# A state-space and attention block on one core: a first stage by half tiles, and all queries ahead of the state-space quarters

## The chip, the cores and the metric

The kernel runs on one core of a Trainium2 chip. The core has five engines with a queue of instructions each: PE (TensorE, the matrix multiplier; its weight loads are listed as PEld), DVE (VectorE), ACT (ScalarE), POOL (GpSimd) and SP (SyncE, which here starts the DMA transfers). An engine works off its own queue in order and waits for others by semaphores. The metric is the device time of one execution, in microseconds (us); less is better.

## The reference, cut to what matters

One transformer-like layer on 512 tokens of width 1024, in float32:

```python
n1 = rmsnorm(h, g_mix)                 # h: 512 x 1024
z = n1 @ w_in                          # columns: ssm 512 | q 512 | kv 768 | gates 24 | merge 2048
y_ssm = s5_mixer(z[..., OFF_SSM:OFF_Q], ...)    # 32 groups of 16 channels, 64 complex states each
y_nsa = nsa_mixer(z[..., OFF_Q:OFF_KV], ...)    # attention: compressed, selected and window branch
merge = sigmoid(z[..., OFF_MERGE:])
mixed = merge[..., :1024] * (y_ssm @ w_br_ssm) + merge[..., 1024:] * (y_nsa @ w_br_nsa)
h = h + mixed @ w_out
h = h + conv_ffn(rmsnorm(h, g_ffn), w_up, conv_w, conv_b, w_down)   # 2 x 2816 wide
gate = sigmoid(rmsnorm(h, g_ple) @ w_ple_gate)
h = h + gate * (p @ w_ple_proj)        # p: 512 x 256, the embedding
return rmsnorm(h, g_final)
```

`s5_mixer` is a linear recurrence over the tokens, `state = a_bar * state + B u`, `y = Re(C state) + d u`, where `a_bar = exp(lambda * dt)` is complex; then come a gelu and a gated product with `w_glu`.

## The kernel before, in words

**Precision.** TensorE multiplies operands in the type fp32r. Each large product is therefore made of three: an operand is split in a high part (a copy to fp32r, on ACT, the function `copy`) and a low part (operand minus high part, on DVE or POOL, the function `tt` with SUB, line L54), and high x high, low x high and high x low are added up in one PSUM bank. So whatever TensorE multiplies needs first an ACT copy and then a subtraction, and the third kind of pass is the one that needs the low weights.

**Memory.** PSUM has eight banks, two each under four names ("acc", "s", "t", "o"). Raw weights of a projection (`wr`, 128x1024) have three buffers, their high and low parts (`wh`, `wl`) two each: splitting a third weight waits until TensorE has finished with the first.

**Who orders what.** Up to L506 the four compute engines follow the order in which the code is written (the block under `tc.manual_schedule`). From there a scheduler orders the instructions of each engine when the program is built; `tc.issue_after(x)` holds work back until instruction x, and the stage leaves such marks: `trig_at` (the last angle operation on DVE), `exp_at` (POOL's last instruction so far) and `zero_at` (ACT's last gate and value copy). DMAs are issued on SP's queue in the order of the code.

**First stage (L240 to L506).**
- *Warm-up*: 12 float32 matmuls of 128x128 without a use for their result. A float32 matmul is two passes, so the trace shows 24.
- *Embedding*: `p @ w_ple_proj` in two halves of 512 columns (`embedded(i, qt)`: half i, 128 tokens qt; six matmuls of 128x512 each, `pje`). `pT` holds the high and low parts of p, `wp[i]` those of half i of the weights (`wpr` raw). `embedded_out` copies a result to SBUF, and later a DMA takes it to DRAM, since it is needed only at the end.
- *Normalization of x*, four tiles of 128 tokens (qt = 0 to 3). `xload(qt)` loads the tile twice: as rows (`rows[qt]`, for the sum of squares) and transposed (`xT`). `squared` is the sum of squares on ACT, `rooted` the power -0.5 on POOL (two instructions, `rx`), `spread` a matmul that spreads the 128 roots over all partitions (`rb`), `x_scaled` eight DVE operations of 128x128 that multiply xT by the gain and by `rb`, `n_high` the high part on ACT (`n1h`, 128x1024) and `n_low` the low part on DVE (`n1l`).
- *Values and gates*: `v_passes(qt, passes)` multiplies a tile with 280 columns of w_in, eight matmuls for each of the three kinds of pass (`vps`). The weights `WV` come in two pieces of 128 and 152 columns (`wv(x, i)`, low parts by `wv_lo`). `v_out` takes the result out: tanh for the gates, high part, low part.
- *Angles*: `angled` is a chain of small DVE operations (128x16, up to 14 of them an exponential) that prepares the state-space parameters; `some(n)` issues the next n of it.
- `u_split` splits the weights of the first two projections.

Row 0 of x lies in one half of a buffer (`wv_101` in the rows below, [:, 1]) whose other half takes the first value weights.

**Projections and quarters.** A projection (`proj`, lines L82 to L84) is 24 matmuls of 128x512 into a bank `pj`. There are four for the state space (`un`; each result goes to DRAM and back in another layout, `ud` and `Uc`), four for the queries (`queries(i)`, result `QT`), then keys and the inputs of the compressed branch. Each needs `wh` and `wl` of one weight block of 512 KB.

The state space is worked off in four quarters of eight groups (`ssm_quarter(q)`). Each makes products of powers and parameters on DVE (`z`) and POOL (`x`), which ACT places in `Z` and `CX`; TensorE transposes Z (`wbps`), ACT copies that (`WB`); TensorE multiplies with `Uc` (`wps`); DVE turns and scans the result (`sr`, with the decay `dec` and the table `tab` that POOL and ACT make once, L631); TensorE makes `tps` out of Z and CX and the output `yps` out of both. Z and CX have two sets of buffers, which alternate between quarters.

Later stages are attention, the state space's gated product (`glu`), merge, FFN and gate. Their code is the same in both kernels.

Of the kernel before, what the change touches and what calls it, by code (L numbers as in the profile page):

```python
# [18 lines left out]
P = 128  # L19
# [25 lines left out]
def hybrid_kernel(ctx: ExitStack, tc: tile.TileContext, A, out):  # L45
# [194 lines left out]

    def xload(qt):
        nc.sync.dma_start(rows[qt], dr("x", qt * P * D, [[D, P], [1, D]]))
        nc.sync.dma_start(xT[:, qt], dr("x_t", qt * P * D, [[D, P], [P, KD], [1, P]]))
# [14 lines left out]
    nc.sync.dma_start(cols, dr("cols", 0, [[NCOLS, P], [1, NCOLS]]))  # L258
    for k in range(2):
        wpload(1, k)  # L260
# [7 lines left out]
    for qt in range(1, NQ):  # L268
        xload(qt)
# [22 lines left out]
    def v_out(qt):  # L292
        ps = vps[qt]
        vv = VV[:, qt].rearrange("p b g x d -> p (b g) x d")
        x = ps[:, 0:256].rearrange("p (a d) -> p a d", d=HD)
        S.activation(gates[:, qt], ps[:, 256:280], AF.Tanh, scale=0.5)
        copy(vv[:, :, 0], x)
        ts(gates[:, qt], gates[:, qt], 0.5, 0.5, MUL, ADD, G)
        tt(vv[:, :, 1], x, vv[:, :, 0], SUB)
# [17 lines left out]
    def x_scaled(qt):  # L317
        for k in range(KD):
            stt(xT[:, qt, k], xT[:, qt, k], gmix[:, k:k + 1], rbp[0][:, qt * P:(qt + 1) * P], MUL, MUL)

    def n_of(qt):
        return (slice(None), slice(None), slice(qt * P, qt * P + P))

    def n_high(qt):
        copy(n1h[n_of(qt)], xT[:, qt])

    def n_low(qt):
        tt(n1l[n_of(qt)], xT[:, qt], n1h[n_of(qt)], SUB)
# [96 lines left out]
    with tc.manual_schedule(engines={mybir.EngineType.PE, mybir.EngineType.Activation, mybir.EngineType.DVE,  # L425
                                    mybir.EngineType.Pool}):
        warm = bank("s", "warm")
        for _ in range(12):
# [7 lines left out]
        for k in range(2):  # L436
# [3 lines left out]
            tt(wp[0][:, 1, k], wpr[:, 0, k], wp[0][:, 0, k], SUB)  # L440
        for k in range(2):
            for n in range(3):
                for qt in range(NQ):
                    embedded(0, qt, (n,), (k,))
        for k in range(2):
            copy(wp[1][:, 0, k], wpr[:, 1, k])
        tt(wp[1][:, 1], wpr[:, 1], wp[1][:, 0], SUB)
        squared(0)
        rooted(0)
        some(11)  # L450
# [4 lines left out]
        x_scaled(0)  # L455
        embedded_out(0, 2)
        copy(*wv(0, 0))
        embedded(1, 1)
        embedded_out(0, 3)
        n_high(0)  # L460
        V.tensor_copy(*wv(0, 1))
        wv_lo(0)
        squared(1)
        rooted(1)
        n_low(0)
        embedded(1, 2)
# [13 lines left out]
        embedded_out(1, 3)  # L480
# [1147 lines left out]
```

## Time and profile before

| | |
|---|---|
| time, median of 3 runs | 824.14 us (823.76 to 824.20) |
| the profiled execution | 823.85 us, of which the span of instructions 822.1 us |
| instructions | 12173 |
| PE busy | 799.3 us, 97% |
| weight loads (PEld) | 673.6 us, 82% |
| DVE busy | 523.6 us, 64% |
| ACT busy | 404.6 us, 49% |
| POOL busy | 246.8 us, 30% |
| granted TensorE clock, mean | 0.993 |
| moved by DMA | 89.70 MB, mean 109 GB/s |

Times in the timeline count from the start of the span. A row of the timeline has start, length, engine, line, operation, output <- inputs, shapes and the number of such instructions in a row; in brackets stands how long the engine stood idle ahead of it and what released it. A row of the waits has the sum, the number and the longest of them. Matmuls overlap one another, so one matmul's length is more than the distance from one to the next.

### The profile page before, as it was taken

To read this page: it belongs to the slowest core of one execution; us is meant where nothing else is said; L and a number is where in the kernel's file an instruction comes from. 1 tells how busy PE (TensorE), PEld (TensorE's weight loads), DVE (VectorE), ACT (ScalarE), POOL (GpSimd) and SP (SyncE) were. 2 spreads that over 40 slices of the span, in tenths; PEclk is the share of its full clock that TensorE was granted. 3 is DMA by queue.
4 is the path that set the end of the run, shared out by engine and by line. 5 is a ranking of instruction groups with operands and counts; after the bars stand their busy time and mean duration, and the time that the engine had idled before them with its cause. 6 is when DMAs were issued, how large, how long until landed. Compare 5 with 4: busy or idle time off the path is not lost. (4 is left out here: it accounts for less than half of the span.)

```text
span 822.1 us, 12173 instructions
## 1 busy us (share of the span) xinstructions
PE 799.3 (97%) x4492; PEld 673.6 (82%) x4492; DVE 523.6 (64%) x1102; ACT 404.6 (49%) x742; POOL 246.8 (30%) x281
## 2 busy tenths in 40 slices
PE   8698999999999999999999999999999999999995
PEld 7586888888888888878898888888888888888884
DVE  5789987765777752197454444554444657998764
ACT  6446464355877754245353443444434433484632
POOL 1468121014655543251022223333333200000321
PEclk9999999999999999999999999999999999999998
DMA  9735222141332512244023333223322352525111
GB/s 348 281 127 143 97 72 65 66 118 62 103 85 71 180 50 79 102 150 157 1 77 104 102 103 103 97 86 100 101 86 94 103 176 81 205 64 167 52 52 51
DMA packets 29707, 89.70 MB, mean 109 GB/s; under 512 B 3664, under 2 KB 5840, under 8 KB 29648
## 3 DMA queue, kind: packets, MB, share of 16 engines
q1 hardware_dynamic: 29072, 87.88, 32.4%
q10 hardware_dynamic: 576, 1.05, 0.3%
q8 instruction: 35, 0.57, 0.3%
q14 instruction: 24, 0.20, 0.1%
HBM read 79.48 MB, written 5.24 MB: 103 GB/s over the span
## 5 line engine op out<-in xcount | busy, mean ns | idle before, releaser
L54 POOL TENSOR_TENSOR wl<-wr,wh 128x1024 fp32r<-128x1024 f32 x39 | 93.8, 2405 | 244.5 <-ACT wh L75 244.4
L75 ACT ACTIVATE wh<-wr 128x1024 fp32r<-128x1024 f32 x88 | 93.2, 1059 | 85.7 <-issue 25.8
L54 DVE TENSOR_TENSOR wl<-wr,wh 128x1024 fp32r<-128x1024 f32 x49 | 64.0, 1306 | 55.9 <-ACT wh L75 55.1
L82 PE MATMUL pj<-n1h,wh 128*128 128x512 f32 x224 | 91.7, 409 | 0.3 <-ACT un L75 0.3
L84 PE MATMUL pj<-n1h,wl 128*128 128x512 f32 x224 | 88.7, 397 | 0.7 <-DVE wl L54 0.7
L83 PE MATMUL pj<-n1l,wh 128*128 128x512 f32 x224 | 88.2, 394 | 0.0
L63 DVE SCALAR_TENSOR_TENSOR cv<-ub,cols,cv 128x511 f32<-128x511 f32 (+1 forms) x44 | 32.9, 748 | 66.2 <-ACT cv L1268 65.4
L83 PE MATMUL ua<-n2l,wh 128*128 128x512 f32 (+1 forms) x176 | 66.9, 380 | 0.2 <-DVE n2l L63 0.2
L82 PE MATMUL ua<-n2h,wh 128*128 128x512 f32 (+1 forms) x176 | 66.9, 380 | 0.0
L84 PE MATMUL ub<-n2h,wl 128*128 128x512 f32 (+1 forms) x176 | 66.8, 379 | 0.0
L83 PE MATMUL ub<-n2l,wh 128*128 128x512 f32 (+1 forms) x176 | 66.8, 379 | 0.0
L84 PE MATMUL ua<-n2h,wl 128*128 128x512 f32 (+1 forms) x176 | 66.8, 379 | 0.0
L82 PE MATMUL ub<-n2h,wh 128*128 128x512 f32 (+1 forms) x176 | 66.8, 379 | 0.0
L84 PEld LDWEIGHTS pj<-n1h,wl 128*128 128x128 f32 x224 | 42.4, 189 | 10.3 <-DVE wl L54 1.0
L82 PEld LDWEIGHTS pj<-n1h,wh 128*128 128x128 f32 x224 | 42.6, 190 | 8.6 <-ACT un L75 0.7
L83 PEld LDWEIGHTS pj<-n1l,wh 128*128 128x128 f32 x224 | 42.6, 190 | 7.6 <-issue 0.4
L60 POOL TENSOR_SCALAR pr<-pr,su,gates 128x512 f32<-128x512 f32 (+1 forms) x64 | 38.9, 616 | 31.4 <-DVE su L988 28.7
L54 DVE TENSOR_TENSOR pl<-ptp,ph 128x128 fp32r<-128x128 f32 (+1 forms) x64 | 31.1, 487 | 14.9 <-ACT ph L75 14.5
L987 ACT ACTIVATE pr<-pr,nb 128x512 f32<-128x512 f32 (+1 forms) x64 | 35.6, 557 | 7.4 <-DVE nb L985 7.2
L54 POOL TENSOR_TENSOR wg1l<-wr,wg1h 128x1024 fp32r<-128x1024 f32 x2 | 4.9, 2434 | 113.5 <-ACT wg1h L75 113.5
L75 ACT ACTIVATE ph<-ptp 128x128 fp32r<-128x128 f32 (+1 forms) x64 | 27.7, 432 | 22.6 <-PE ptp L996 22.1
L83 PEld LDWEIGHTS ua<-n2l,wh 128*128 128x128 f32 x176 | 33.1, 188 | 6.7 <-DVE n2l L63 0.4
(477 smaller groups left out, 2067.6 us busy)
## 6 DMA issues: line engine op xcount, KB each, us to landing
wr<-in_w_up_dram SPq DMA_DIRECT2D x44, 512.0 KB, 3.5
wr<-in_w_in_dram SPq DMA_DIRECT2D x28, 512.0 KB, 3.4
b<-in_w_down_dram SPq DMA_DIRECT2D x14, 512.0 KB, 3.6
QQ<-QT SPq DMA_DIRECT2D x16, 256.0 KB, 3.6
wr<-in_w_out_dram SPq DMA_DIRECT2D x8, 512.0 KB, 3.5
wr<-in_w_down_dram SPq DMA_DIRECT2D x8, 512.0 KB, 4.5
wr<-in_w_ple_gate_dram SPq DMA_DIRECT2D x8, 512.0 KB, 3.5
xT<-in_x_t_dram SPq DMA_DIRECT2D x4, 512.0 KB, 9.7
```

The source lines that it names most:

```text
L54: e.tensor_tensor(o, a, b, op=op)
L60: e.tensor_scalar(o, a, s1, s2, op0=op0, op1=op1)
L63: e.scalar_tensor_tensor(o, a, s, b, op0=op0, op1=op1)
L75: S.activation(o, a, AF.Copy)
L82: PE.matmul(ps, lh, rh, start=start, stop=False)
L83: PE.matmul(ps, lh, rl, start=False, stop=False)
L84: PE.matmul(ps, ll, rh, start=False, stop=stop)
L987: S.activation(pp, pp, AF.Exp, bias=nb, scale=-1.0, accum_out=su)
```

## The change: loads, the first stage's order, and the queries' place

The change has three parts.

*Loads.* `xload` is cut in two: `rowload` (rows) and `xload` (transposed). Rows 0 and 1 are loaded ahead of the second half of the embedding weights, rows 2 and 3 ahead of their transposed tiles as before.

*First stage.* Six warm matmuls instead of twelve. The squares and roots of tiles 0 and 1 stand ahead of the second embedding weights' split. `x_scaled` and `n_high` work on halves of 512 columns in turn (`normed_tile`); `n_low` stays whole. The second value weights' high part moves from DVE to ACT (`copy(*wv(0, 1))` for `V.tensor_copy`). `spread` stands ahead of the previous tile's value passes. `v_out` becomes `v_high` and `v_low`, which stand further back; the rest of the angles (`some(50)`) moves behind tile 3 and the first low weights.

*Behind it.* All four queries are written ahead of the quarters, the compressed inputs stand behind quarter 0, the keys behind quarter 1, the compression behind quarter 2.

```diff
+    def rowload(qt):
+        nc.sync.dma_start(rows[qt], dr("x", qt * P * D, [[D, P], [1, D]]))
+
     def xload(qt):
-        nc.sync.dma_start(rows[qt], dr("x", qt * P * D, [[D, P], [1, D]]))
         nc.sync.dma_start(xT[:, qt], dr("x_t", qt * P * D, [[D, P], [P, KD], [1, P]]))
...
+    for qt in range(2):
+        rowload(qt)
     for k in range(2):
         wpload(1, k)
     xload(0)
...
-    for qt in range(1, NQ):
+    xload(1)
+    for qt in range(2, NQ):
+        rowload(qt)
         xload(qt)
...
-    def v_out(qt):
-        ps = vps[qt]
+    def v_high(qt):
+        S.activation(gates[:, qt], vps[qt][:, 256:280], AF.Tanh, scale=0.5)
+        x, hi, _ = v_parts(qt)
+        copy(hi, x)
+        ts(gates[:, qt], gates[:, qt], 0.5, 0.5, MUL, ADD, G)
...
+    def v_low(qt):
+        x, hi, lo = v_parts(qt)
+        tt(lo, x, hi, SUB)
...
-    def x_scaled(qt):
-        for k in range(KD):
+    def x_scaled(qt, half):
+        for k in range(4 * half, 4 * half + 4):
             stt(xT[:, qt, k], xT[:, qt, k], gmix[:, k:k + 1], rbp[0][:, qt * P:(qt + 1) * P], MUL, MUL)
...
+    def normed_tile(qt):
+        for half in range(2):
+            x_scaled(qt, half)
+            n_high(qt, half)
...
-        for _ in range(12):
+        for _ in range(6):
             PE.matmul(warm[:, :P], ident, root, start=True, stop=True)
...
+        squared(0)
         for k in range(2):
             for n in range(3):
                 for qt in range(NQ):
                     embedded(0, qt, (n,), (k,))
+        rooted(0)
+        some(16)
+        squared(1)
+        rooted(1)
         for k in range(2):
             copy(wp[1][:, 0, k], wpr[:, 1, k])
-        tt(wp[1][:, 1], wpr[:, 1], wp[1][:, 0], SUB)
-        squared(0)
-        rooted(0)
-        some(11)
+            tt(wp[1][:, 1, k], wpr[:, 1, k], wp[1][:, 0, k], SUB)
         for qt in range(2):
             embedded_out(0, qt)
         embedded(1, 0)
         spread(0)
-        x_scaled(0)
+        embedded(1, 1)
+        x_scaled(0, 0)
+        n_high(0, 0)
         embedded_out(0, 2)
+        x_scaled(0, 1)
+        n_high(0, 1)
+        embedded_out(0, 3)
+        embedded(1, 2)
+        n_low(0)
         copy(*wv(0, 0))
-        embedded(1, 1)
-        embedded_out(0, 3)
-        n_high(0)
-        V.tensor_copy(*wv(0, 1))
         wv_lo(0)
-        squared(1)
-        rooted(1)
-        n_low(0)
-        embedded(1, 2)
+        copy(*wv(0, 1))
         wv_lo(1)
...
-        v_passes(0, (0,))
         spread(1)
-        x_scaled(1)
-        v_passes(0, (1, 2))
-        embedded_out(1, 2)
+        v_passes(0, (0, 1))
         squared(2)
         rooted(2)
-        n_high(1)
+        normed_tile(1)
+        v_passes(0, (2,))
         n_low(1)
...
+        spread(2)
         v_passes(1, (0,))
-        spread(2)
-        x_scaled(2)
         squared(3)
         rooted(3)
-        n_high(2)
+        normed_tile(2)
         v_passes(1, (1, 2))
-        v_out(0)
         n_low(2)
+        v_high(0)
+        u_split(0, 0)
+        exp_at = last(mybir.EngineType.Pool)
+        spread(3)
+        v_passes(2, (0,))
+        normed_tile(3)
+        v_passes(2, (1, 2))
+        n_low(3)
+        v_high(1)
+        v_low(0)
+        v_low(1)
+        u_split(0, 1)
         some(50)
         trig_at = last(mybir.EngineType.DVE)
-        exp_at = last(mybir.EngineType.Pool)
-        u_split(0, 0)
-        spread(3)
-        x_scaled(3)
-        v_passes(2, (0, 1, 2))
-        n_high(3)
-        n_low(3)
-        v_out(1)
-        u_split(0, 1)
         u_split(1, 0)
...
-    queries(0)
-    queries(1)
+    for i in range(4):
+        queries(i)
     for q in range(4):
         ssm_quarter(q)
         if q == 0:
-            queries(2)
-            queries(3)
-        elif q == 1:
             compress_in(0)
             compress_in(1)
-        elif q == 2:
+        elif q == 1:
             keys(0)
             keys(1)
-    compress(0)
-    VC = compress(1)
+        elif q == 2:
+            compress(0)
+            VC = compress(1)
```

How the instructions stand on three engines, before and after (line, operation, output <- input, shape; x8 is eight in a row):

SP's queue behind the first embedding weights, before: each tile's rows stand directly ahead of its transposed tile.

```order
L258 DMA cols<-in_cols_dram 128x284
L253 DMA wpr<-in_w_ple_proj_dram 128x512 x2
L242 DMA wv_101<-in_x_dram 128x1024
L243 DMA xT<-in_x_t_dram 128x1024
L267 DMA wv_101<-in_w_v_dram 128x1024
L267 DMA wv_128<-in_w_v_dram 128x1216
L242 DMA row_102<-in_x_dram 128x1024
L243 DMA xT<-in_x_t_dram 128x1024
```

The same place on SP's queue in the changed kernel:

```order
L260 DMA cols<-in_cols_dram 128x284
L242 DMA wv_101<-in_x_dram 128x1024
L242 DMA row_102<-in_x_dram 128x1024
L255 DMA wpr<-in_w_ple_proj_dram 128x512 x2
L245 DMA xT<-in_x_t_dram 128x1024
L271 DMA wv_101<-in_w_v_dram 128x1024
L271 DMA wv_129<-in_w_v_dram 128x1216
L245 DMA xT<-in_x_t_dram 128x1024
```

Rows 0 and 1 have moved up past the second embedding weights, and row 1 also past xT of tile 0 and both value weights.

TensorE from the first value pass to that of tile 2, before (L315 is a spread, L289 value passes; n1h x WV high, n1l x WV high, n1h x WV low):

```order
L289 MATMUL vps<-WV,n1h 128x280 x8
L315 MATMUL rb<-root,rx 128x128
L289 MATMUL vps<-WV,n1l 128x280 x8
L289 MATMUL vps<-WV,n1h 128x280 x16
L315 MATMUL rb<-root,rx 128x128
L289 MATMUL vps<-WV,n1l 128x280 x8
L289 MATMUL vps<-WV,n1h 128x280 x8
L315 MATMUL rb<-root,rx 128x128
L289 MATMUL vps<-WV,n1h 128x280 x8
```

The same place on TensorE in the changed kernel:

```order
L326 MATMUL rb<-root,rx 128x128
L295 MATMUL vps<-WV,n1h 128x280 x8
L295 MATMUL vps<-WV,n1l 128x280 x8
L295 MATMUL vps<-WV,n1h 128x280 x8
L326 MATMUL rb<-root,rx 128x128
L295 MATMUL vps<-WV,n1h 128x280 x8
L295 MATMUL vps<-WV,n1l 128x280 x8
L295 MATMUL vps<-WV,n1h 128x280 x8
L326 MATMUL rb<-root,rx 128x128
L295 MATMUL vps<-WV,n1h 128x280 x8
```

A spread now stands ahead of all three passes of the tile before it, where it stood behind the first of them.

ACT around the table `tab` (two instructions at L631, before), between the projections and the first quarters. Each `wh` is one projection's high weights, `un` and `QT` take results out:

```order
L629 ACTIVATE tab_610<-SIN 128x16
L75 ACTIVATE wh<-wr 128x1024
L75 ACTIVATE un<-pj 128x512
L631 ACTIVATE tab_609<-tab_609 128x16x31
L631 ACTIVATE tab_610<-tab_610 128x16x31
L75 ACTIVATE wh<-wr 128x1024
L75 ACTIVATE dec<-rho_89 128x256
L75 ACTIVATE un<-pj 128x512
L75 ACTIVATE Z_809<-z_915 64x16x16 x2
L75 ACTIVATE Z_810<-z_922 64x16x16 x2
```

The same place on ACT in the changed kernel, where the table is L653:

```order
L651 ACTIVATE tab_609<-SIN 128x16
L75 ACTIVATE wh<-wr 128x1024
L75 ACTIVATE un<-pj 128x512
L75 ACTIVATE wh<-wr 128x1024
L75 ACTIVATE un<-pj 128x512
L653 ACTIVATE tab_608<-tab_608 128x16x31
L653 ACTIVATE tab_609<-tab_609 128x16x31
L75 ACTIVATE dec<-rho_89 128x256
L75 ACTIVATE Z_808<-z_980 64x16x16 x2
L75 ACTIVATE wh<-wr 128x1024
L75 ACTIVATE QT<-pj 128x512
L75 ACTIVATE Z_809<-z_987 64x16x16 x2
```

Two more projections' weights are split ahead of the table than before, and two more results (`un`, the third and fourth) are taken out ahead of it.

More of the change, by code (lines that the diff above doesn't have):

```diff
@@ L290, in v_passes, with v_parts @@
                           stop=n == 2 and k == KD - 1)
-    def v_out(qt):
-        ps = vps[qt]
-        vv = VV[:, qt].rearrange("p b g x d -> p (b g) x d")
[L295 to L299, printed above, removed]
+    def v_high(qt):
[3 more added lines that the diff above has]
+        ts(gates[:, qt], gates[:, qt], 0.5, 0.5, MUL, ADD, G)
+    def v_parts(qt):
+        vv = VV[:, qt].rearrange("p b g x d -> p (b g) x d")
+        return vps[qt][:, 0:256].rearrange("p (a d) -> p a d", d=HD), vv[:, :, 0], vv[:, :, 1]
+    def v_low(qt):
+        x, hi, lo = v_parts(qt)
+        tt(lo, x, hi, SUB)
     def squared(qt):
@@ L315, in spread, with n_of, n_high @@
         PE.matmul(rbp[0][:, qt * P:(qt + 1) * P], rx[qt].to_broadcast([P, P]), root, start=True, stop=True)
-    def x_scaled(qt):
-        for k in range(KD):
+    def x_scaled(qt, half):
+        for k in range(4 * half, 4 * half + 4):
             stt(xT[:, qt, k], xT[:, qt, k], gmix[:, k:k + 1], rbp[0][:, qt * P:(qt + 1) * P], MUL, MUL)
[L321 to L325, printed above, removed]
-    def n_low(qt):
-        tt(n1l[n_of(qt)], xT[:, qt], n1h[n_of(qt)], SUB)
+    def n_of(qt, half):
+        ks = slice(4 * half, 4 * half + 4)
+        return (slice(None), ks, slice(qt * P, qt * P + P)), xT[:, qt, ks]
+    def n_high(qt, half):
+        o, x = n_of(qt, half)
+        copy(n1h[o], x)
+    def n_low(qt):
+        o = (slice(None), slice(None), slice(qt * P, qt * P + P))
+        tt(n1l[o], xT[:, qt], n1h[o], SUB)
+    def normed_tile(qt):
+        for half in range(2):
+            x_scaled(qt, half)
+            n_high(qt, half)
     uw = []
@@ L470, in hybrid_kernel @@
             embedded_out(1, qt)
-        v_passes(0, (0,))
         spread(1)
-        x_scaled(1)
-        v_passes(0, (1, 2))
-        embedded_out(1, 2)
+        v_passes(0, (0, 1))
         squared(2)
         rooted(2)
-        n_high(1)
+        normed_tile(1)
+        v_passes(0, (2,))
         n_low(1)
-        embedded_out(1, 3)
+        for qt in (2, 3):
+            embedded_out(1, qt)
+        spread(2)
         v_passes(1, (0,))
-        spread(2)
-        x_scaled(2)
         squared(3)
         rooted(3)
-        n_high(2)
+        normed_tile(2)
         v_passes(1, (1, 2))
-        v_out(0)
         n_low(2)
+        v_high(0)
[10 more added lines that the diff above has]
+        u_split(0, 1)
         some(50)
         trig_at = last(mybir.EngineType.DVE)
-        exp_at = last(mybir.EngineType.Pool)
-        u_split(0, 0)
-        spread(3)
-        x_scaled(3)
-        v_passes(2, (0, 1, 2))
-        n_high(3)
-        n_low(3)
-        v_out(1)
-        u_split(0, 1)
         u_split(1, 0)
@@ L503, in hybrid_kernel @@
         for qt in (2, 3):
-            v_out(qt)
+            v_high(qt)
+            v_low(qt)
         zero_at = last(mybir.EngineType.Activation)
```

## The prediction

> **What bounds the kernel now.** I read TensorE's waits over the whole span, then busy time by stretches, and then the timeline of the first 82 us.
>
> ```profile
> PE vps L289 <- ACT n1h L75: 5.3, 3, 3.5
> ...
> PE wbps L715 <- ACT Z L75: 1.8, 1, 1.8
> ...
> PE pj L82 <- ACT un L75: 0.3, 1, 0.3
> ...
> 18.80:43.30 24.50, 16.25 (x103) 14.90 (x102) 18.32 (x56) 11.53 (x25) 12.79 (x34) 0.93 0.70 271
> 43.30:65.70 22.40, 22.10 (x100) 18.01 (x98) 21.52 (x73) 11.33 (x21) 15.89 (x42) 1.00 0.49 147
> 65.70:69.60 3.90, 1.37 (x7) 0.70 (x7) 3.83 (x6) 0.83 (x2) 3.90 (x9) 0.98 0.17 68
> 69.60:82.00 12.40, 12.40 (x49) 10.04 (x50) 10.72 (x14) 10.08 (x20) 9.16 (x10) 0.87 0.50 149
> 82.00:160.00 78.00, 78.00 (x901) 66.06 (x899) 65.12 (x133) 35.99 (x65) 13.27 (x16) 1.00 0.23 73
> ```
>
> In a row of waits stand the sum, the number and the longest; in a row of a stretch its length, the busy time of PE, PEld, DVE, ACT and POOL, and TensorE's granted clock. TensorE is the bound, and nearly all that it waits for lies ahead of 70 us: it is busy 16.25 us of 24.5 while the value tiles are made (18.8 to 43.3), and there is a second hole at 65 to 70. From 82 to 160 it is never free. So microseconds saved ahead of 70 move all that follows, unless a new wait eats them.
>
> The first stage, row by row:
>
> ```profile
> 2.17 5.49 PE L429 MATMUL warm<-root,ident 128*128 128x128 f32 x24 [2.17 <-POOL mt L520]
> 4.31 0.63 ACT L75 ACTIVATE wp<-wpr 128x512 fp32r<-128x512 f32 x1
> 7.32 1.50 PE L411 MATMUL pje<-wp,pTh 128*128 128x512 f32 x4
> 8.65 1.08 PE L411 MATMUL pje<-wp,pTl 128*128 128x512 f32 x4
> 9.57 1.99 PE L411 MATMUL pje<-wp,pTh 128*128 128x512 f32 x8
> 14.61 0.38 PE L315 MATMUL rb<-root,rx 128*128 128x128 f32 x2
> 15.03 2.16 DVE L63 SCALAR_TENSOR_TENSOR xT<-xT,cols,rb 128x128 f32<-128x128 f32 x8 [2.76 <-PE rb L315]
> 18.95 1.22 DVE L54 TENSOR_TENSOR n1l<-xT,n1h 128x1024 fp32r<-128x1024 f32 x1
> 19.41 2.16 POOL L58 TENSOR_SCALAR rx<-ss 128x1 f32<-128x1 f32 x1
> 22.19 0.22 POOL L58 TENSOR_SCALAR rx<-ss 128x1 f32<-128x1 f32 x1
> 22.27 0.49 PE L315 MATMUL rb<-root,rx 128*128 128x128 f32 x2 [2.05 <-POOL rx L54]
> 22.52 1.28 PE L289 MATMUL vps<-WV,n1l 128*128 128x280 f32 x8
> 24.98 1.06 ACT L75 ACTIVATE n1h<-xT 128x1024 fp32r<-128x1024 f32 x1 [2.91 <-DVE xT L63]
> 33.55 0.17 DVE L54 TENSOR_TENSOR th<-cols,dt 128x16 f32<-128x16 f32 x1
> 35.33 0.17 DVE L63 SCALAR_TENSOR_TENSOR kk<-rd,kk 128x16 f32<-128x16 f32 x1
> 38.72 2.23 PE L289 MATMUL vps<-WV,n1h 128*128 128x280 f32 x8 [3.50 <-ACT n1h L75]
> 43.45 0.39 PE L82 MATMUL pj<-n1h,wh 128*128 128x512 f32 x1
> 43.68 0.39 PE L83 MATMUL pj<-n1l,wh 128*128 128x512 f32 x1
> ```
>
> One tile's chain is square (ACT), root (POOL), spread (PE), scaling (DVE, 2.16), high part (ACT, 1.06), low part (DVE, 1.22), value passes (PE). Tile 1's root took 2.16 us instead of 0.22 beside DVE's two-tensor subtractions, and TensorE stood 2.05. Tile 3's scaling stood behind the angle operations (33.55 to 35.4, ten of them), and TensorE stood 3.50. The first projection begins at 43.45; its matmuls start 0.23 us apart, so a projection of 24 takes 5.45.
>
> **The change, step by step.** *Start.* There are six warm matmuls fewer, 12 of 24 passes. The 24 took 5.1 us until the next work, so 12 end at 4.8, and the first weights are split at 4.94 (4.31 + 0.63). The embedding begins at 5.0 instead of 7.3. Four 512-wide matmuls took 1.33 us up to 8.65 and 0.92 after it: TensorE ran slow until about 8. With 0.43 a matmul until 8.0 and 0.23 after, the 24 of the first half end at 11.8 instead of 13.2: 1.4 us gained. On SP's queue two rows for the squares now go ahead of the second embedding weights. At 414 GB/s (first row below) one of 512 KB is 1.27 us, so these weights land 2.5 us later, at about 10.9, and ACT, which squares both rows first, has split them by 12.2, DVE's low part by 12.9. TensorE wants them one after the other from 11.8 to 13: just in time, at worst 1 us late. xT of tile 0 lands at 4.54 + 6.3 + 1.3 = 12.1, ahead of the spread, which comes at 13.2 instead of 14.6. What follows on the queue carries the same bytes as before.
>
> ```profile
> 7.30:18.80 11.50, 11.50 (x51) 9.40 (x51) 7.42 (x23) 7.00 (x11) 0.81 (x2) 1.00 1.02 414
> ...
> 4.54 0.43 SPq L243 DMA_DIRECT2D xT<-in_x_t_dram  x1
> ...
> DMA to landing us min/median/max: 6.3/9.7/10.3
> ...
> 80.54 0.58 ACT L75 ACTIVATE QT<-pj 128x512 fp32r<-128x512 f32 x1
> ```
>
> *Tiles.* By halves, scaling is 1.08 + 1.08 and each 512-wide high part 0.6 (the QT row), so the high part is whole 0.6 after the scaling instead of 1.1. ACT also takes WV's second high part (1.25, from 1.06 for 1024 columns to 1216), done at 19.3, and the first value pass waits for it from 18.0; DVE's cast of that part goes. Passes of eight take 1.1 each. Tile 0: low part 17.6, low parts of WV 20.7, passes 19.3 to 22.7. Tile 1: scaling 20.7 to 22.9, low part 23.5 to 24.7, passes end 27.0. Tile 2: scaling 24.7 to 26.9, ACT's two CT copies hold its second half by 0.3, low part 27.7 to 28.95, passes end 31.15. Tile 3: scaling to 31.1, low part 31.7 to 32.95, passes end 35.15. The roots of tiles 2 and 3 (0.8 each) fall beside scaling, not beside two-tensor subtractions, and end before TensorE is free for the spread. The values' low parts no longer stand ahead of a tile's low part: two of them (0.35 each) and the first projection's low weights (1.15) follow tile 3 on DVE and end at 34.8. So projections begin at **35.2 instead of 43.45: 8.2 us**. Waits left are 1.3 at 18.0 and 0.6 twice. If ACT, which carries squares, copies and halves in one row, slips 0.6 a tile, 2 us of it go; if the short waits vanish, 1 us comes on top.
>
> *Projections and quarters.*
>
> ```profile
> 58.11 1.71 DVE L54 TENSOR_TENSOR wl<-wr,wh 128x1024 fp32r<-128x1024 f32 x1
> 62.38 0.62 ACT L631 ACTIVATE tab<-tab 128x496 f32<-128x496 f32 x1 [6.49 <-POOL tab L54]
> 63.79 1.05 ACT L75 ACTIVATE wh<-wr 128x1024 fp32r<-128x1024 f32 x1
> 67.66 1.88 DVE L54 TENSOR_TENSOR wl<-wr,wh 128x1024 fp32r<-128x1024 f32 x1
> 69.59 0.79 PE L84 MATMUL pj<-n1h,wl 128*128 128x512 f32 x1 [0.73 <-DVE wl L54]
> 71.46 0.63 PE L82 MATMUL pj<-n1h,wh 128*128 128x512 f32 x1
> 71.89 0.63 PE L83 MATMUL pj<-n1l,wh 128*128 128x512 f32 x1
> 73.27 0.39 PE L84 MATMUL pj<-n1h,wl 128*128 128x512 f32 x1
> 70.77 0.84 ACT L75 ACTIVATE Z<-z 64x256 f32<-64x256 f32 x2 [2.62 <-DVE z L54]
> 71.64 0.95 ACT L75 ACTIVATE CX<-x 64x320 f32<-64x320 f32 x2
> ```
>
> Before, ACT waits 6.49 for POOL's table, so the first query's high weights come at 63.79 and its low ones at 67.66, behind products for the quarters. TensorE waits 0.3 + 1.8 + 0.7 = 2.8 and then starts a matmul each 0.43 until about 72.7: 3.1 us at half rate, 1.6 lost. Together 4.4.
>
> After, ACT makes two queries' weights ahead of the table. DVE's work from 43.5 to 65.1 (21.6, without a gap) grows by what now stands behind the start (the angles 1.9, and 1.5 for six more of 0.25) and by two low weights (1.7 and 1.8): 28.5. From 34.8, with 0.5 to 1 for waiting on ACT's weights, it ends at 63.9 to 64.3. The second query starts at 35.2 + 5 x 5.45 = 62.45 and needs its low weights at the third matmul, 62.9: a wait of 1.0 to 1.4. After the third query (75.4) TensorE needs the copy WB. Ahead of it on ACT, from DVE's next z at 72.7, stand Z 0.84, CX 0.95, wh 1.05, QT 0.6, Z 0.84 and WB itself 0.6: 77.6, a wait of 2.2. With 0.4 for shorter ones I count 4.0 in all, against 4.4: a gain of 0.4. The other queries' low weights are ready 0.5 or more ahead. None of these waits is longer than about the 2.05 at 22.27, after which eight value matmuls took 1.28, the full rate; the half rate came after the 3.50, and after the stretch 65.7 to 69.6 with 1.37 busy of 3.90. So I cost the clock at nothing.
>
> The Trainium skill, "TensorE: Matmul & The Clock Gate", Part 1, has the clock halved after an idle window of about 3.4 us. By that rule neither new wait halves it and the sum stays; the rows here agree. If a wait of 2.2 did halve it, the sum would be 1.6 us more.
>
> From 43.5 to 160 DVE is busy 21.5 + 3.8 + 10.7 + 65.1 = 101 of 116.5. Its slack of 15.4 loses 3.4 (angles) and at most 4.4 (the shorter span), so DVE doesn't bound the quarters as a whole. Compression, moved behind the third quarter, and keys, behind the second, leave less for TensorE beside the last scan chain; I cost it at nothing, since two gate projections (10.9) stand there. Without that cover it would be 3 us.
>
> The sum: the profiled execution, 823.85 (0.3 below the median 824.14), less 8.2, less 0.4: **815.2 us**.
>
> **Rivals.** (a) *No new waits in the quarters*, if DVE's work there runs at 1.2 a weight instead of 1.7 to 1.9: 823.85 - 8.2 - 4.4 = 811.2. Against it: POOL starts its table only after DVE's cosines, so both still work side by side. (b) *The quarters give back half.* TensorE arrives 8 us earlier at a DVE that has 3.4 more to do, and waits some 4 us more than I count: 819. For it: DVE's 21.52 busy of 22.4 just there. (c) *No effect*: something other than TensorE sets the time later, or the quarters return all. Against it: 78 of 78 us busy, and it would need all 8.6 lost: 823.9. (d) *Slower: the clock stays at half rate through the value passes*, kept there by their short waits. The 96 value matmuls take 0.14 each, and at half rate 13 us more; from 75 of them (10.3 us) on, the kernel is slower by over 0.2%; with all, 828. Against it: the row at 22.52. The same page of the Trainium skill, in "A second HAM failure mode: psum-queue depth-cycling", tells of a clock that oscillates under frequent short idling; the trace does not bear it out, since it shows full rate there with waits of 2.05 and less.
>
> **How the numbers follow.** My forecast (813 to 817.3) has a chance of 0.52, (a) 0.17, (b) 0.22, (c) 0.05, (d) 0.04. The range of 811.0 to 819.3 takes in most of (a) and two thirds of (b), 0.8 in all; its ends are the sum without a wait in the quarters, and with half the gain returned. 0.2% of this kernel is 1.65 us, about what a measurement tells from no change. Faster 0.91, same 0.05, slower 0.04.
>
> **What would show it.** The first projection starts at about 35 (at 38 or later the tile steps are wrong). No root of 2 us on POOL ahead of a spread. TensorE waits 1 to 2 us on low weights at the second query and about 2 on WB near 76, and for nothing longer than 3. Behind 100 us the same matmuls stand some 9 us earlier. It is wrong if matmuls start 0.43 apart after 10 us, or if TensorE waits for DVE's sr between the quarters.

## The result, and the profile after

The changed kernel takes 813.42 us (median of 4 runs, 812.94 to 814.34); the kernel before takes 823.95 in the same comparison (4 runs, 822.17 to 824.20). The ratio is 0.9878, with a 95% interval of 0.9861 to 0.9895. The forecast was 815.2, between 811.0 and 819.3. The profiled execution took 813.89, 10.0 less than the 823.85 of before.

TensorE's waits in the changed kernel, the six largest behind the warm-up (sum, number, longest):

```profile
PE vps L295 <- DVE n1l L54: 1.3, 3, 0.5
PE pj L84 <- DVE wl L54: 1.2, 1, 1.2
PE vps L295 <- ACT WV L75: 1.0, 1, 1.0
PE pje L430 <- ACT wp L75: 0.8, 1, 0.8
PE wps L745 <- ACT WB L75: 0.8, 1, 0.8
PE pj L82 <- DVE QT L54: 0.6, 1, 0.6
```

The 3.5, the 2.0 and the 1.8 of before are gone. What is left is one wait for the second embedding weights (0.8), short ones in the value tiles, and three between the second query and the first quarter (`wl`, `QT`, `WB`).

Busy time by stretches of the changed kernel (length, PE, PEld, DVE, ACT and POOL busy, granted clock, share and GB/s of the DMA):

```profile
7.30:18.80 11.50, 10.38 (x45) 7.78 (x43) 8.82 (x30) 8.35 (x15) 1.83 (x6) 1.00 1.02 411
18.80:35.20 16.40, 14.09 (x100) 13.07 (x101) 14.13 (x35) 12.22 (x27) 7.75 (x18) 1.00 1.03 383
35.20:62.40 27.20, 27.20 (x122) 22.56 (x121) 24.79 (x89) 13.25 (x23) 18.55 (x53) 1.00 0.56 186
62.40:78.00 15.60, 13.00 (x61) 10.02 (x60) 14.11 (x19) 9.22 (x18) 11.73 (x16) 1.00 0.28 85
78.00:160.00 82.00, 82.00 (x923) 70.06 (x923) 67.55 (x147) 39.44 (x73) 17.61 (x20) 1.00 0.24 75
```

The value tiles take 16.4 us with 14.1 busy, where before they took 24.5 with 16.25; the clock is 1.00 in each stretch, where before it was 0.93 in the value tiles and 0.87 from 69.6 to 82. The clock's record in the trace of the kernel before has two stretches at half rate, 38.74 to 42.15 and 69.46 to 72.87; the changed kernel's has none between 5.78 and 807.91. Half rate for 6.8 us costs at most 3.4, so up to a third of the 10.0 is clock and not waiting.

The timeline of the changed kernel, mostly at the places that the prediction names:

```profile
5.00 1.54 PE L430 MATMUL pje<-wp,pTh 128*128 128x512 f32 x4
6.38 1.09 PE L430 MATMUL pje<-wp,pTl 128*128 128x512 f32 x4
11.93 0.50 PE L430 MATMUL pje<-wp,pTh 128*128 128x512 f32 x1 [0.83 <-ACT wp L75]
13.70 0.38 PE L326 MATMUL rb<-root,rx 128*128 128x128 f32 x2
19.53 1.29 PE L295 MATMUL vps<-WV,n1h 128*128 128x280 f32 x8 [1.02 <-ACT WV L75]
21.58 0.22 POOL L58 TENSOR_SCALAR rx<-ss 128x1 f32<-128x1 f32 x1 [3.11 <-ACT row L313]
23.73 1.23 DVE L54 TENSOR_TENSOR n1l<-xT,n1h 128x1024 fp32r<-128x1024 f32 x1 [0.70 <-ACT n1h L75]
35.26 0.39 PE L82 MATMUL pj<-n1h,wh 128*128 128x512 f32 x1
60.51 0.62 ACT L653 ACTIVATE tab<-tab 128x496 f32<-128x496 f32 x1 [1.91 <-POOL tab L54]
64.30 0.50 PE L84 MATMUL pj<-n1h,wl 128*128 128x512 f32 x1 [1.22 <-DVE wl L54]
69.44 1.04 PE L737 MATMUL wbps<-ident,Z 128*128 128x128 f32 x8
71.08 0.50 PE L82 MATMUL pj<-n1h,wh 128*128 128x512 f32 x1 [0.60 <-DVE QT L54]
77.62 0.60 PE L745 MATMUL wps<-Uc,WB 128*128 128x128 f32 x3 [0.79 <-ACT WB L75]
171.72 0.48 PE L82 MATMUL glu<-ys,wh 128*128 128x512 f32 x1
```

The first projection starts at 35.26 instead of 43.45, 8.19 earlier. The first matmul of the gated product (`glu`) starts at 171.72. The same instruction of the kernel before:

```profile
181.71 0.48 PE L82 MATMUL glu<-ys,wh 128*128 128x512 f32 x1
```

So 9.99 are gained by there, 8.19 ahead of the projections and 1.80 behind; the end of the span has moved by 10.0 too (822.1 to 812.1), so nothing is lost or won after it.

### The profile page after: what moved, and what is told of

Read it like the earlier page. It is cut to its first block, busy times and chain, and to the rows that moved or that the text cites. A ratio compares the mean times of both kernels' runs of the same rounds, so it can differ in the third digit from the quotient of the medians.

```text
span 812.1 us, 12156 instructions
## 1 busy us (share of the span) xinstructions
PE 794.4 (98%) x4480; PEld 668.9 (82%) x4480; DVE 520.1 (64%) x1102; ACT 405.5 (50%) x747; POOL 246.6 (30%) x281
## 5 line engine op out<-in xcount | busy, mean ns | idle before, releaser
L84 PEld LDWEIGHTS pj<-n1h,wl 128*128 128x128 f32 x224 | 42.0, 188 | 11.1 <-DVE wl L54 1.6
```

What stands on the lines that cost most here:

```text
L84: PE.matmul(ps, ll, rh, start=False, stop=stop)
```

## The experiments

Each kernel was timed beside runs of the kernel before on the same chip. The medians of the kernel before differ between these comparisons by up to 2 us, so kernels are compared by their ratios, and smaller differences by the traces. "First projection" and "first glu" are the starts of these two matmuls in the profiled execution, and "half rate" is the time that the clock's record in its trace shows at 0.5, without the start-up and the last 8 us. One execution of each kernel was profiled. Kernels with the same order of work up to the first projection differ there by several tenths (35.06, 35.26 and 35.67 in stage_only, after and angles_later; 42.98 and 43.45 in queries_only and before), so smaller differences between two traces say little.

| kernel | median us | before beside it | ratio, 95% interval | first projection | first glu | span | half rate, us |
|---|---|---|---|---|---|---|---|
| before | 823.95 | | | 43.45 | 181.71 | 822.1 | 6.8 |
| after | 813.42 | 823.95 | 0.9878, 0.9861 to 0.9895 | 35.26 | 171.72 | 812.1 | 0 |
| stage_only | 814.25 | 823.53 | 0.9886, 0.9871 to 0.9901 | 35.06 | 171.91 | 812.4 | 0 |
| queries_only | 824.06 | 823.53 | 1.0010, 1.0000 to 1.0019 | 42.98 | 181.76 | 822.3 | 6.8 |
| before_angles_late | 819.23 | 822.00 | 0.9958, 0.9943 to 0.9974 | 38.95 | 177.00 | 817.5 | 0 |
| angles_early | 823.01 | 823.53 | 0.9994, 0.9984 to 1.0004 | 36.69 | 178.24 | 821.5 | 6.8 |
| angles_early_tab_late | 823.62 | 822.00 | 1.0011, 1.0001 to 1.0021 | 38.35 | 176.93 | 820.0 | 3.4 |
| angles_early_pin | 821.69 | 822.15 | 0.9984, 0.9974 to 0.9993 | 38.70 | 179.47 | 820.0 | 6.8 |
| angles_later | 816.38 | 821.92 | 0.9922, 0.9905 to 0.9939 | 35.67 | 171.62 | 817.0 | 3.4 |
| whole_tiles | 814.79 | 823.53 | 0.9895, 0.9879 to 0.9910 | 36.75 | 172.53 | 813.0 | 0 |
| warm0 | 814.23 | 822.00 | 0.9901, 0.9883 to 0.9919 | 35.88 | 172.31 | 812.8 | 0 |
| low_halves | 812.19 | 822.15 | 0.9874, 0.9858 to 0.9891 | 33.32 | 169.37 | 809.8 | 0 |
| best2 | 810.26 | 822.00 | 0.9851, 0.9835 to 0.9868 | 32.88 | 169.22 | 809.7 | 0 |
| best3 | 810.18 | 822.15 | 0.9854, 0.9836 to 0.9871 | 31.55 | 167.61 | 808.1 | 0 |

### Which half of the change does it: stage_only and queries_only

stage_only keeps the changed first stage and writes queries, keys and compression where they stood before:

```diff
-    for i in range(4):
-        queries(i)
+    queries(0)
+    queries(1)
     for q in range(4):
         ssm_quarter(q)
         if q == 0:
+            queries(2)
+            queries(3)
+        elif q == 1:
             compress_in(0)
...
```

> The changed first stage, with queries, compression and keys written where they stood before. Theory: the gain of 10.0 us in the profiled executions is made by the first stage alone, 8.2 by the earlier first projection (35.26 instead of 43.45) and 1.8 because the weights of two queries now stand ahead of the table on ACT; in this kernel's instruction order they stand there too, so the place of the queries in the code is not what does it: 813 to 815 us, and no wait of ACT of 6 us on the table that holds up a query. Rival: the parts add up, the queries' place gives the 1.8: 815.5 to 816.5.

queries_only is the other half: the kernel before with only this last part of the change.

> The first stage of before, with all queries ahead of the quarters, compression and keys moved as in the change. Theory: without the earlier first stage ACT still waits some 6.5 us on POOL's table ahead of the first query's weights, TensorE waits 2.8 us and runs slow for 3 us as before: 822.5 to 824.5 us, no change. Rival: the queries' place is worth 1.8 us by itself: 822 or less.

ACT's first wide table instruction in stage_only, and the same in queries_only:

```profile
60.43 0.62 ACT L653 ACTIVATE tab<-tab 128x496 f32<-128x496 f32 x1 [2.04 <-POOL tab L54]
```

```profile
61.60 0.62 ACT L631 ACTIVATE tab<-tab 128x496 f32<-128x496 f32 x1 [6.15 <-POOL tab L54]
```

The first stage alone gives the gain (0.9886 against 0.9878, intervals nearly the same; first glu 0.19 later, within what executions differ by), and the place of the queries alone gives none (1.0010). The 1.80 us behind the projections belong to the first stage too: with its order the scheduler puts six weights ahead of ACT's table, as in the changed kernel, while without it ACT waits 6.15 as before, although all queries are written first. Both kernels did what the theory said.

### The place of the angles: before_angles_late, angles_early and three more

before_angles_late is the kernel before with one edit:

```diff
         n_low(2)
-        some(50)
-        trig_at = last(mybir.EngineType.DVE)
         exp_at = last(mybir.EngineType.Pool)
...
         u_split(0, 1)
+        some(50)
+        trig_at = last(mybir.EngineType.DVE)
         u_split(1, 0)
```

> The kernel before, with one edit: the rest of the angles and their mark moved behind tile 3 and the first low weights. Theory: the wait of 3.50 ahead of tile 3 falls to 1.6, the slow value passes behind it (4.7 us for 24 and 8 instead of 3.4) run at the full rate, so the first projection starts at 40 to 40.5 instead of 43.45; and ACT makes six weights ahead of the table, which takes away 1.5 to 2.5 us of waits and slow matmuls behind 65: 818 to 820 us, about half of the change's gain from one moved line. Rival: halves of tiles, early rows and early spreads carry the gain, and the angles' place gives at most their own 1.9: 821.5 to 822.5.

The time is as expected, and the first projection came at 38.95, a little ahead of the expected 40 to 40.5. By its ratio, 0.9958, this one edit gives a third of the change's gain, by the first glu nearly half (4.71 of 9.99). The rest of the first stage is worth the other 3.7 us of first projection. No run separates its parts (early rows, early spreads, fewer warm matmuls) except the halves, below.

angles_early undoes that edit in the changed kernel:

```diff
         v_high(0)
+        some(50)
+        trig_at = last(mybir.EngineType.DVE)
         u_split(0, 0)
...
         u_split(0, 1)
-        some(50)
-        trig_at = last(mybir.EngineType.DVE)
         u_split(1, 0)
```

> The changed kernel, with the rest of the angles ahead of tile 3's scaling, as before the change, instead of behind it. Theory: ten operations (1.9 us) delay tile 3's low part, TensorE waits about 1.9 us more ahead of its low passes (one wait of 2 to 2.4 on n1l or on n1h), the first projection comes at 37.1; the table comes up to 2 us earlier, which takes the waits at the second query (1.2) and WB (0.8) away at most: 813.5 to 815.5 us. Rival: the angles hide in DVE's waits for ACT (0.7 a tile): first projection by 35.8, 812 to 813.

The first projection came at 36.69, 1.4 late where some 1.9 was expected, but the whole gain was gone: 0.9994. The rest lies behind. ACT's table in angles_early, what TensorE waits for, and a wait in attention:

```profile
58.01 0.62 ACT L653 ACTIVATE tab<-tab 128x496 f32<-128x496 f32 x1 [8.29 <-POOL tab L54]
```

```profile
63.89 0.79 PE L84 MATMUL pj<-n1h,wl 128*128 128x512 f32 x1 [3.05 <-DVE wl L54]
64.48 0.63 PE L82 MATMUL pj<-n1h,wh 128*128 128x512 f32 x1
192.88 0.50 PE L1028 MATMUL ops<-PTC,VC 128*128 128x512 f32 x1 [1.69 <-DVE PTC L54]
```

With the angles early the scheduler put a table instruction ahead of the fifth projection's weights on ACT (the first query's), their low part came at 63.8, and the matmuls behind ran 0.43 apart until 69.6 (clock at half rate from 63.08 to 69.91). From the first glu to the end of the span it took 643.3 instead of 640.4, with a wait in attention that the changed kernel does not have. Three more kernels were to tell which of these is the cause.

angles_early_tab_late pins ACT's table behind the fourth state-space result (`issue_after` around the four table instructions):

> The changed kernel with the angles ahead of tile 3's scaling, as in angles_early, but with ACT's four table instructions pinned behind the result of the fourth state-space projection. Theory: angles_early lost 9.6 us because its earlier mark let the scheduler put one table instruction ahead of a projection's weights on ACT (a wait of 8.29, then TensorE waiting 3.05 and a slow stretch), and the angles themselves cost only the later first projection, 36.7 instead of 35.3: 814.5 to 816 us, no wait of TensorE over 2 us. Rival: the angles ahead of tile 3 crowd DVE so that the loss comes whatever ACT's order is: 820 or more.

The theory fell. The table no longer stood in the way, and the time stayed at 1.0011 (the profiled execution, 821.67, is 2.0 below the median). DVE and TensorE in this kernel:

```profile
61.56 0.82 DVE L54 TENSOR_TENSOR z<-PR,bb 128x256 f32<-128x256 f32 x1
62.31 0.51 DVE L54 TENSOR_TENSOR z<-PI,bb 128x256 f32<-128x256 f32 x1
62.74 1.21 DVE L54 TENSOR_TENSOR wl<-wr,wh 128x1024 fp32r<-128x1024 f32 x1
64.01 0.50 PE L84 MATMUL pj<-n1h,wl 128*128 128x512 f32 x1 [3.21 <-DVE wl L54]
```

ACT had these weights' high part at 55.75 (54.69 and 1.06), but DVE took the rest of the coefficients (`kr`, `ki`, `bb`) and the first two products ahead of the low part, which it began at 62.74. In the changed kernel the fifth low weights stand at 53.48 and the sixth at 62.49, just ahead of the products.

angles_early_pin leaves only the mark `trig_at` late, with the angles early:

> The changed kernel with the angles ahead of tile 3's scaling, as in angles_early, but with the mark trig_at, behind which the scheduler may start the products that follow the angles, left at its late place. Theory: what made angles_early lose 9 us beyond the 1.4 of the first projection is the mark: with it early, the scheduler put the products on DVE one place ahead of the low weights (five low weights ahead of bb's products instead of six), and TensorE waited 3.05. With the late mark six stand ahead or beside them: first projection at 36.7 to 38.4 (the later, if TensorE runs slow after the wait ahead of tile 3), waits behind it at most 3 in all: 815 to 817.5 us. Rival: the angles in front of tile 3 are themselves what disturbs everything behind: 820 or more.

This theory fell too: 0.9984, as its rival had it. The wait at the low weights became 1.12, but TensorE waited 3.23 on a query's result later, and it ran at half rate twice. Two waits and the stretches of 2 us around the slow places in angles_early_pin:

```profile
62.20 0.50 PE L84 MATMUL pj<-n1h,wl 128*128 128x512 f32 x1 [1.12 <-DVE wl L54]
78.31 0.50 PE L82 MATMUL pj<-n1h,wh 128*128 128x512 f32 x1 [3.23 <-DVE QT L54]
```

```profile
34.00:36.00 2.00, 1.52 (x7) 1.29 (x8) 2.00 (x4) 1.60 (x5) 1.78 (x3) 0.67 1.04 411
36.00:38.00 2.00, 2.00 (x11) 2.00 (x9) 1.52 (x4) 0.00 (x0) 1.78 (x5) 0.50 0.20 76
80.00:82.00 2.00, 2.00 (x6) 1.61 (x5) 1.52 (x1) 2.00 (x5) 1.84 (x3) 0.50 0.00 0
```

angles_later puts angles and mark one step further back, behind the second low weights:

> The changed kernel with the angles and their mark put back further, behind the second low weights. Theory: what counts behind the first stage is how far DVE's chain of angles and products runs ahead of TensorE's projections: where it starts earlier against the first projection, its block of products comes one low weight sooner and TensorE waits for that weight. Here it starts later, so the wait at the second query's low weights (1.2) goes, and the products, Z and WB come up to 1.5 later, so the waits there (0.6 and 0.8) grow by 1 to 2: first projection at 35.3 as in the changed kernel, 812.8 to 814.5 us, no gain and no loss of note. Rival: later is better, as the low weights are what TensorE waits for: 811.5 to 812.5.

The waits moved as expected (the second query's 1.22 went, Z took 0.82), and the first glu came at 171.62, level with the changed kernel. But the time, 816.38, lies above both the theory's range and its rival's. From the first glu on it took 645.4 instead of 640.4 in the profiled execution (its median is 2.4 lower than that execution), with a wait of 1.68 for PTC at the place where angles_early has 1.69: the order of attention, 110 us further on, had come out differently. Behind this wait the clock was at half rate from 187.22 to 190.63, which it was not in angles_early and angles_early_tab_late behind theirs of 1.69.

What the five show: the angles' place is worth 9 to 11 us in the changed kernel by the ratios of the three kernels with early angles. How that splits can be read from the profiled executions, in us against the changed kernel:

| kernel | first projection later | from there to first glu | behind first glu | together | more waits of TensorE | at half rate |
|---|---|---|---|---|---|---|
| angles_early | 1.4 | 5.1 | 2.9 | 9.4 | 4.8 | 6.8 |
| angles_early_tab_late | 3.1 | 2.1 | 2.7 | 7.9 | 4.0 | 3.4 |
| angles_early_pin | 3.4 | 4.3 | 0.2 | 7.9 | 3.6 | 6.8 |
| angles_later | 0.4 | -0.5 | 5.0 | 4.9 | 1.3 | 3.4 |

Longer waits, and at most half of the time at half rate, make up 5.7 to 8.2 of the 7.9 to 9.4 in the first three; the rest is not assigned. The three with early angles have the same order in the first stage, and what sets their first projections apart (1.4 against 3.1 and 3.4) is mainly half rate at tile 3, which angles_early did not have there. What stays open is why each wait stands where it does, since the scheduler orders DVE, ACT and TensorE anew up to attention. Common to the three with early angles is that TensorE stood for low weights (1.12 to 3.21) near 61 us, behind four projections and two matmuls, where the changed kernel came to such a wait near 63, behind five and two. All loss behind the first glu comes with the wait for PTC: angles_early_pin and the changed kernel don't have it.

### The size of the pieces: whole_tiles, low_halves, warm0

whole_tiles makes one high part of 1024 columns again:

```diff
         for half in range(2):
             x_scaled(qt, half)
-            n_high(qt, half)
+        n_high(qt)
```

> The changed kernel, with one high part of 1024 columns behind the whole scaling instead of two of 512. Theory: a tile goes round on DVE (scaling 2.15, wait for the high part 0.7, low part 1.2) and TensorE waits for it; the whole high part makes the wait 1.1 to 1.2 instead of 0.7, four times 0.45: the first projection at 36.7 to 37.1 instead of 35.26, 815 to 815.5 us. Rival: TensorE's passes bound the tiles, so nothing moves by more than 0.5: 813.4 to 814.

DVE's wait ahead of a low part in whole_tiles:

```profile
24.48 1.22 DVE L54 TENSOR_TENSOR n1l<-xT,n1h 128x1024 fp32r<-128x1024 f32 x1 [1.12 <-ACT n1h L75]
```

It is 1.12 instead of 0.70, the round of a tile 4.41 both times instead of 3.99 and 4.09 (scaling to scaling, from 21.21 to 25.62 to 30.03 against 20.89 to 24.88 to 28.97), and the first projection 1.49 later. The first glu is 0.81 later: about half of what the tiles lose is made good in the quarters, where the waits are 2.2 in sum instead of 2.6. The ratio, 0.9895, can't be told from 0.9878, and the median, 814.79, lies just under the expected 815.

low_halves goes on in the same direction, with the low part in halves too:

```diff
     def n_low(qt):
-        o = (slice(None), slice(None), slice(qt * P, qt * P + P))
-        tt(n1l[o], xT[:, qt], n1h[o], SUB)
+        for half in range(2):
+            o, x = n_of(qt, half)
+            tt(n1l[o], x, n1h[o], SUB)
```

> The changed kernel with each tile's low part on DVE in two halves, nothing else. Theory: a tile's round on DVE (scaling 2.15, wait 0.7 for the high part, low part 1.2) loses its wait and becomes 3.5, as long as TensorE's own 24 passes and spread (3.45 to 3.6); the three waits on low parts (1.3 in all) go: the first projection at 33.8 to 34.2 instead of 35.26, 811.8 to 813 us. Rival: the second query's low weights and WB are tied to the table and not to the first stage, so the 1.3 is waited for there: 813 to 814.

```profile
20.64 2.15 DVE L63 SCALAR_TENSOR_TENSOR xT<-xT,cols,rb 128x128 f32<-128x128 f32 x8
22.70 1.48 DVE L54 TENSOR_TENSOR n1l<-xT,n1h 128x512 fp32r<-128x512 f32 x2
24.10 2.15 DVE L63 SCALAR_TENSOR_TENSOR xT<-xT,cols,rb 128x128 f32<-128x128 f32 x8
```

The first low half fills the time in which ACT makes the second high half, and a round takes 3.46, the next one 3.66 (24.10 to 27.76, with a wait of 0.30). The first projection came at 33.32, 1.94 earlier than in the changed kernel and 0.5 ahead of the theory, and the first glu 2.35 earlier: the quarters gave nothing back. The theory held against its rival by the trace; the ratio 0.9874 alone would not tell.

warm0 leaves out the warm matmuls:

> The changed kernel without warm matmuls. In the kernel before and in the changed one the full rate came about 0.9 us after the embedding's first matmul (at 8.2 and at 5.9). Theory A: so the warm matmuls do nothing for it, and it comes at about 5.9 here too: 813.0 to 813.8 us. Theory B: the rate rises some 3.7 us or more after TensorE's first work of any kind: the embedding runs at 0.43 a matmul until 8.6 or later, its first half ends 1.6 later, of which the wait for the second weights (0.83) takes a part: 0.5 to 1 us slower, 813.9 to 814.5.

The embedding's start in warm0:

```profile
4.89 2.08 PE L430 MATMUL pje<-wp,pTh 128*128 128x512 f32 x4 [4.89 <-ACT wp L75]
6.77 1.91 PE L430 MATMUL pje<-wp,pTl 128*128 128x512 f32 x4
8.47 2.78 PE L430 MATMUL pje<-wp,pTh 128*128 128x512 f32 x8
11.09 1.07 PE L430 MATMUL pje<-wp,pTl 128*128 128x512 f32 x4
```

Eight matmuls take 3.58 (4.89 to 8.47) and the next eight 2.62, so the full rate comes near 10 (10.14 by the clock's record). Theory B held for the clock: the warm matmuls count, since in the ten kernels with six of them the full rate came between 5.05 and 8.16. What that is worth is not settled. The first projection is 0.62 later than in the changed kernel and the first glu 0.59, but angles_later, with the warm matmuls, has its first projection only 0.21 ahead of warm0's; the ratio, 0.9901, can't be told from 0.9878.

### A version that is faster than both: best2 and best3

best2 adds to low_halves an earlier first spread, and loads and squares row 1 later:

```diff
-    for qt in range(2):
-        rowload(qt)
+    rowload(0)
     for k in range(2):
         wpload(1, k)
     xload(0)
+    rowload(1)
...
-        squared(1)
-        rooted(1)
         for k in range(2):
             copy(wp[1][:, 0, k], wpr[:, 1, k])
             tt(wp[1][:, 1, k], wpr[:, 1, k], wp[1][:, 0, k], SUB)
         for qt in range(2):
             embedded_out(0, qt)
-        embedded(1, 0)
+        squared(1)
+        rooted(1)
         spread(0)
+        embedded(1, 0)
```

> The changed kernel with more of the same: low parts by halves too, row 1 loaded behind xT of tile 0, the second embedding weights split ahead of row 1's square, the first spread ahead of the second half of the embedding. Theory: TensorE's remaining waits ahead of the first projection (0.83 for weights, 1.02 for WV, 1.3 for low parts) come from ACT's and DVE's rows; a tile's round on DVE falls from 4.05 to about 3.45, and the first projection starts at 33 to 34; what follows on DVE moves with it: 811.5 to 812.7 us. Rival: the second query's low weights and WB come when POOL's table and DVE's products are done, and waits there grow by what was gained: 813 to 814.

best3 moves the spread of tile 1 ahead of the last embedding, half of its scaling ahead of WV's low parts, and WV's high parts ahead of one embedding result:

> best2, with the spread of tile 1 ahead of the last embedding, the first half of tile 1's scaling ahead of the value weights' low parts, and the value weights' high parts ahead of one embedding result on ACT. Theory: the wait of 0.64 on WV and of 0.30 ahead of the spread go, and DVE's 0.74 ahead of WV's low part is filled: first projection at 32.0 to 32.4 instead of 32.88, 809 to 810 us. Rival: the quarters' waits grow by as much: 810 to 811.

Both have lower ratios than the change, 0.9851 and 0.9854 (the medians, 810.26 and 810.18, stand beside lower ones of before than the change's does). Their intervals overlap with 0.9861 to 0.9895, so the times alone don't tell them from it; the traces do (first glu at 169.22 and 167.61 instead of 171.72). Of best2's 2.5 us by that measure, low_halves alone has 2.35, so for row 1's place and the earlier spread 0.15 is left, less than executions differ by. best2 came out below its expected range (811.5). best3's first projection, at 31.55, is earlier than expected, and its wait for WV stayed at 0.61, now for the low part. Its time lies where the rival had it, but the rival's reason, longer waits in the quarters, did not come: its first glu is 1.61 earlier than best2's, its first projection 1.33.

## Why the prediction was right, point by point

- **Tiles, 8.2 us: right.** Forecast 35.2, measured 35.26; that it fits to 0.1 is luck, since executions with the same order came at 35.06 to 35.67. Its pieces are less exact. A tile was to go round in 4.0 to 4.2 us, and did (23.73 to 27.82 from low part to low part, then 4.00). The wait of 1.3 for WV was 1.02, and the two of 0.6 were three of 0.34 to 0.48. No root took 2 us: the one at 21.58 took 0.22.
- **Start: the clock was wrong, without effect.** "TensorE ran slow until about 8" is no fixed time. In the changed kernel four matmuls took 1.38 and the next four 0.92 (6.38 to 7.30), so the full rate came near 6, and the embedding's first half ended at 11.1 for the forecast 11.8; in low_halves, with the same work up to there, it came at 8.16. TensorE then waited 0.83 for the second weights, inside the "at worst 1 us late", and the spread came at 13.70 for 13.2. It doesn't show at 35.26, since the first value pass waited for WV on ACT, which was done near 19.5 for the forecast 19.3.
- **Quarters, 0.4 us: the term that was mis-sized.** It was 4.4 less 4.0; measured is 4.4 less 2.6 (1.22, 0.60 and 0.79), so 1.8. The failed step is the sum of the waits. The places and the ends were right: the low weights at the second query (forecast 63.9 to 64.3, measured 64.30) and WB (77.6, measured 77.62). By the prediction's own times, though, TensorE has work up to 74.4: 35.2, seven projections of 5.45, and the eight transposes (1.04 at 69.44). So no more than 3.2 could be waited up to 77.6. The 75.4 that it set against 77.6 holds only some 1.0 of the first wait, while the sum counts 1.4 for it, 0.4 for shorter ones and still the full 2.2. A wait that ends at a fixed time gets shorter by what TensorE has waited ahead of it. Of the 3.2, 2.6 showed as waits; the other 0.6 is in matmuls that started further apart behind the waits (0.33 instead of 0.23 for the first).
- **What makes it: not told apart.** The prediction had ACT making two queries' weights ahead of the table, and did not say which part of the change causes that. stage_only and queries_only show that it is the first stage, and before_angles_late that the angles' place in it is enough: with that one edit six weights stand ahead of the table.
- **The angles' place: far undersized.** The prediction had it as 1.9 us of work that moves on DVE, and nothing else. Undone alone it takes back all of the gain, most of it behind the first projection.
- **Clock in the quarters, nothing: right.** The granted clock is 1.00 in all five stretches. The rule on idle windows of the Trainium skill ("TensorE: Matmul & The Clock Gate", Part 1), by which the sum stayed, and this trace agree: the longest wait behind 35 us is 1.22. The ground that the prediction gave, full rate behind a wait of 2.05, does not hold in general: half rate followed a wait of 2.05 in queries_only and one of 1.68 in angles_later.
- **Rivals.** (b), half of the gain returned in the quarters, and (c), no effect, did not come. (d), half rate in the value passes, did not come in the changed kernel: its first eight took 1.29 at 19.53. (a), no waits in the quarters, at 811.2, is 2.2 off and the forecast 1.8: the measured 813.4 lies between the two, since the quarters' waits were 2.6 where (a) has none and the forecast 4.0.

## What to carry to other kernels

Where one engine is bound nearly everywhere, look for the few microseconds in which it is not, and follow the chain that feeds it there; halving a step so that the next engine starts on its first half paid twice here, once in the change (1.49 us of first projection) and once beyond it (1.94). When you add up waits that end at fixed times, add the last end and not the waits. And where a scheduler orders what follows, undo each moved line by itself: the place of ten small operations decided some 9 us here, by what the scheduler made of it, which no sum of their durations would have told.

## What the runs showed of the hardware

The traces record the clock that TensorE was granted. In all fourteen, every stretch at full rate between start-up and end lasts a whole multiple of 3.41 us (27.31 and 30.72, for instance), and every stretch at half rate between them 3.41 or, once, 6.83. So the clock changes on a grid of 3.41 us, and the grid lies differently against the kernel in each execution.

The full rate came at 5.78 in the changed kernel, at 8.02 in the kernel before and at 10.14 in warm0: 3.6, 5.9 and 5.2 us after TensorE's first work (2.17, 2.17 and 4.89). No number of matmuls or time after the first one fits all three. The Trainium skill, "TensorE: Matmul & The Clock Gate", Part 1, has a free-running window of about 3.4 us behind it; the three values lie between one and two such windows, which agrees. The 2.9 of angles_early (2.18 to 5.05) lies under one.

Half rate does not need one long wait. angles_early_pin, then angles_early, at tile 3:

```profile
32.97 0.78 PE L295 MATMUL vps<-WV,n1h 128*128 128x280 f32 x4 [1.34 <-ACT n1h L75]
34.01 0.79 PE L295 MATMUL vps<-WV,n1h 128*128 128x280 f32 x4 [0.25 <-ACT n1h L75]
35.27 2.23 PE L295 MATMUL vps<-WV,n1l 128*128 128x280 f32 x8 [0.47 <-DVE n1l L54]
```

```profile
32.09 0.78 PE L295 MATMUL vps<-WV,n1h 128*128 128x280 f32 x4 [1.32 <-ACT n1h L75]
33.13 0.79 PE L295 MATMUL vps<-WV,n1h 128*128 128x280 f32 x4 [0.26 <-ACT n1h L75]
34.53 1.30 PE L295 MATMUL vps<-WV,n1l 128*128 128x280 f32 x8 [0.61 <-DVE n1l L54]
```

The waits are almost the same, 2.06 and 2.19 in sum, within some 3.6 us; in the one kernel eight matmuls then took 2.23, in the other 1.30, the full rate. angles_early_tab_late, with the same first stage as angles_early, waited 2.22 there and took 2.06. And behind the wait of 3.23 at 78.31 in angles_early_pin the half rate began only at 79.17.

Where the waits fall on the grid counts. The kernel before and queries_only share two waits near 67 us (1.80 and 1.81 for Z, 0.73 for low weights). Here are the stretches of the grid around them, first of before, then of queries_only:

```profile
66.05:69.46 3.41, 1.01 (x6) 0.42 (x4) 3.34 (x6) 0.83 (x2) 3.41 (x7) 1.00 0.20 77
```

```profile
63.41:66.83 3.42, 2.22 (x9) 1.24 (x7) 3.32 (x6) 1.72 (x4) 3.42 (x10) 1.00 0.30 107
66.83:70.24 3.41, 2.07 (x10) 1.61 (x11) 3.34 (x5) 0.77 (x3) 2.88 (x3) 1.00 0.12 20
```

In the kernel before one stretch takes in both, TensorE is busy for 1.01 of its 3.41 us, and half rate follows at 69.46. In queries_only the grid parts them, 2.22 and 2.07 are busy, and the full rate stays. So a wait of 2 us, in pieces or whole, may cost up to 1.7 us (half of 3.41) or nothing, and the prediction's comparison of single waits was too simple. How much of a stretch has to be busy these traces don't settle: half rate followed stretches with 1.62 to 1.82 busy (angles_later up to 187.22, angles_early_pin up to 34.70), and didn't follow others with 1.59 to 1.82 (angles_early_tab_late up to 65.60, angles_early up to 192.79).
